# A list scheduler's cost model is rewritten: the same 16,310 instructions in another order

## The chip, the cores and the metric

One program runs on one core of a Trainium2 chip. The metric is the device time of one execution in microseconds (us). The engines are TensorE (PE, its weight loads shown as PEld), VectorE (DVE), ScalarE (ACT), GpSimd (POOL) and SyncE (SP). Each engine works through its own instructions in the order in which the program has them; an instruction whose operands are late holds up all that stand behind it on that engine.

## The reference

One layer over 512 latent tokens and 256 context tokens, width 2048, batch 1. An adaLN-modulated RMSNorm is followed by one input projection, whose columns feed two groups of heads; both groups are gated, joined and sent through one output projection.

```python
mod = silu(c) @ w_ada + b_ada                       # shift, scale, gate; also for c_ctx
xn  = rms(x) * norm_g * (1 + scale) + shift
p   = xn @ w_in                                     # 2048 x 6912 (latent and context rows)
# group A, 16 heads x 64: bidirectional RWKV-7, state S (64 x 64) per head and direction
S   = S * w_t - (S @ kk_t) (kk_t * a_t)^T + v_t k_t^T ;  y_t = S @ r_t
# group B, 16 query / 4 key heads x 64: attention in a window of 128, plus all context keys, one sink
o   = softmax([q k_window, q k_ctx, sink]) @ [v_window, v_ctx]
out = x + gate * (concat(groupnorm(y)*silu(z_r), o*silu(z_a)) @ w_out)
```

## The kernel before

**Tiles and stages.** Tokens lie along the free dimension, channels on the 128 partitions; w_in is cut into 54 column tiles of 128 and w_out into 16. A weight part (4 of a tile's 16 row blocks, 128x512) is loaded into a buffer `wf`, rounded by ACT to `whi`, and DVE writes the rest to `wlo` (`split`); there are two `whi` and two `wlo`. Each of the four blocks then costs three products (whi*xh, whi*xl, wlo*xh), on 512 latent columns and, for the first 22 tiles, on 256 context columns too.
- *Lockstep* (0 to 256 us): w_ada and x arrive, 8 column tiles are projected, the row norms are formed.
- *Context units* (to 610 us): 8 pairs of heads, one unit of 256 tokens each, beside the projection of tiles 8 to 21.
- *Latent units* (to 1322 us): 8 pairs, two units of 256 tokens each, beside the projection of tiles 22 to 53; then the norm and rotary of q and k.
- *Attention* (to 1598 us): 8 pairs of heads, beside the first two quarters and most of the third of the output projection.
- *End*: the fourth quarter, which needs all heads, and 16 finished tiles.

A unit is a chain over the engines: `prep` (decays and scaled keys on POOL, ACT, DVE), `stacks` (64-token products on PE, masked by DVE into `ar`), `relay_out`/`solve` (a triangular system of 31 steps on DVE, with DMAs before and after), `levels` (32x32 and 64x64 products on PE) and `scan`, four steps in which PE, DVE and PE take turns. Matmuls of units use parts of the PE array (modes 32x32, 64x64, 64x128, 128x64), those of projections all of it (128x128).

**What sets the order.** All instructions are first recorded with their dependences (`Program.add`, `touch`). `order` then plays them through a model: each engine has a time at which it is free, each instruction a duration (`estimate`) and a rank (the longest modelled path to the end), and an edge between engines costs `AFTER[p.eng] + BEFORE[o.eng]`. On every engine the ready instruction with the highest rank goes next. The instructions are emitted in the order of their modelled starts, and so the model's numbers fix what stands in front of what.

Projection matmuls are *fills* (`o.fill`): on PE their rank is lowered by `FB`, so that a unit's matmul goes first when it is ready within `LOOK` ns of the first possible start. Five fills in a row (`GRP`) are a group that is kept together. If fewer than `COLMIN` columns were streamed in the last `TICK` ns, a fill goes first. Fills are in a fixed order among themselves. The helper that emits records one line for all: L500 before, L536 after.

Of the kernel before, what the change touches and what calls it, by code (L numbers as in the profile page):

```python
# [183 lines left out]
LAT = BOTH + """  # L184
# [74 lines left out]
class Op:  # L259


    __slots__ = ("n", "eng", "f", "a", "k", "dur", "ldw", "twice", "move", "fill", "group", "prev", "next", "left",
                 "ready", "at", "end", "rank", "cols", "small")


class Area:
# [46 lines left out]
class Program:  # L313
# [19 lines left out]
    def add(self, eng, f, a, k):  # L333
        o = Op()
        o.n, o.eng, o.f, o.a, o.k, o.fill = len(self.ops), eng, f, a, k, self.fill
        o.prev, o.next, o.ready, o.ldw, o.twice, o.move = {}, [], 0.0, 0.0, False, 0.0
# [11 lines left out]
        if eng == "scalar" and f == "dma_start":  # L348
            o.dur = 400
        if eng == "tensor":  # L350
            o.small = bool(k.get("tile_position"))
# [12 lines left out]
    def touch(self, o, ap, write):  # L364
# [4 lines left out]
        for i in area.parts:  # L369
            seen = self.seen.setdefault((ap.name, i), ([], []))  # L370
            for w in (False, True) if write else (True,):
                keep = []
                for n, x in seen[w]:
                    if n != o.n and area.meets(x):
                        p = self.ops[n]
                        if p.eng != o.eng or (w and not write and o.eng != "tensor"):
                            lat = self.AFTER[p.eng] + self.BEFORE[o.eng]
                        else:
                            lat = 0
                        o.prev[n] = max(o.prev.get(n, 0), lat)  # L380
                        own = True
                    if not (write and area.covers(x)):
                        keep.append((n, x))
                seen[w][:] = keep
            seen[write].append((o.n, area))
        if held:
            assert held.next is None, ap.name
            if held.last and not own:
                for n in held.last.users:
                    if n != o.n:  # L390
                        p = self.ops[n]
                        lat = self.AFTER[p.eng] + self.BEFORE[o.eng] if p.eng != o.eng else 0
                        o.prev[n] = max(o.prev.get(n, 0), lat)
            held.users.append(o.n)

    def estimate(self, o, outs, ins):
        f, n = o.f, max(size(x) for x in outs[:1] + ins)
        bank = any(x.space == PSUM for x in ins)
        if o.eng == "sync":
            x = outs[0]  # L400
            some = x.shape[0] == 32 and x.space != DRAM and (size(x) > 256 or len(x.ap) > 2)
            o.dur = 625 if x.shape[0] == 64 or some else 450
            row = int(x.ap[-1][1])
            o.move = max(180, math.prod(x.shape) * 4 / (360 if row >= 128 else 240))
        elif o.eng == "tensor":
            m, n = (size(o.k["lhsT"]), size(o.k["rhs"])) if f == "matmul" else (size(ins[0]), size(ins[1]))
            fast = f == "matmul" and ins[0].dtype != F32
            o.twice = f == "matmul" and not fast
            o.dur, o.ldw = n * (0.417 if fast else 0.834), m * 0.834
            o.cols = n * ins[0].shape[0] / 128 * (2 if o.twice else 1)  # L410
            if self.tied and ins[0].shape[0] == 64:
                o.dur /= 2
                o.ldw /= 2
            if o.k.get("tile_position") and o.twice:
                if m == 32 and n >= 128:
                    o.twice, o.dur = False, 0.417 * n + 21
                else:
                    o.twice, o.dur = False, 0.834 * n + (28 if m == 64 else 10)
        elif o.eng == "vector":
            fast = f in ("tensor_copy", "tensor_scalar") and not bank  # L420
            o.dur = 68 + (0.52 if fast else 1.04) * n
            if (f in ("scalar_tensor_tensor", "tensor_scalar")
                    and any(isinstance(x, bass.AP) and size(x) == 1 for x in o.a[2:])):
                o.dur += 60
        elif o.eng == "scalar":
            o.dur = (52 if bank else 94) + 0.834 * n + (93 if "accum_out" in o.k else 0)
            o.dur += 93 * sum(isinstance(o.k.get(x), bass.AP) for x in ("scale", "bias")) if f == "activation" else 0
        else:
            o.dur = {"memset": 36 + 0.84 * n, "tensor_scalar": 160 + 0.84 * n, "tensor_copy": 125 + 3.3 * n}.get(
                f, 150 + 2.1 * n)  # L430

    def order(self):
        ops = self.ops
        for o in ops:
            for n in o.prev:
                ops[n].next.append(o.n)
            o.left = len(o.prev)
        for o in reversed(ops):
            o.rank = o.dur * (2 if o.twice else 1) + (o.move + 650 if o.move else 0)
            o.rank += max((ops[n].prev[o.n] + ops[n].rank for n in o.next), default=0)  # L440
        free = dict.fromkeys(self.AFTER, 0.0)
        begun = moved = 0.0
        group, small, recent, cols = None, False, deque(), 0.0
        avail = {e: [] for e in free}
        for o in ops:
            if not o.left:
                avail[o.eng].append(o)
        key = lambda o: ((o.eng != "tensor") * o.fill, o.rank - (FB if o.fill and o.eng == "tensor" else 0), -o.n)
        done = 0
        while done < len(ops):  # L450
            t, e = min((max(free[e], min(o.ready for o in l)), e) for e, l in avail.items() if l)
            if e == "tensor":
                for o in avail[e]:
                    o.at = max(free[e], max(begun, o.ready) + o.ldw)
                x = min(o.at for o in avail[e]) + LOOK
# [3 lines left out]
                busy = [o for o in avail[e] if o.fill and o.at <= x + FWAIT] if cols < COLMIN else []  # L459
# [3 lines left out]
                group, small = o.group, o.small  # L463
# [5 lines left out]
            o.at = max(t, o.ready)  # L469
            if e == "tensor":  # L470
                o.at = max(free[e], max(begun, o.ready) + o.ldw)
                begun, o.end = o.at, o.at + o.dur
                if o.twice:
                    begun = max(o.end, o.at + o.ldw)
                    o.end = begun + o.dur
                elif o.k.get("tile_position"):
                    begun = o.end - 20
                free[e] = o.end
            elif e == "sync":
                free[e] = o.at + o.dur  # L480
                moved = max(moved, free[e] + 650) + o.move
                o.end = moved
            else:
                free[e] = o.end = o.at + o.dur
# [18 lines left out]

TICK, COLMIN, FWAIT, FB, LOOK, GRP = 3413, 4000, 0, 80000, 30, 5


class Pool:
# [1204 lines left out]
```

## Time and profile before

| | |
|---|---|
| median of 3 runs | 1680.74 us (1673.76 to 1681.35) |
| profiled execution | 1677.45 us, span 1675.6 us |
| PE / DVE / ACT / POOL busy | 1556.3 (93%) / 1319.0 (79%) / 716.6 (43%) / 404.0 (24%) |
| PE granted clock, mean | 0.98 of full speed |
| matmuls recorded | 12454, of 9288 PE instructions (fp32 ones run as two) |

The share of PE is that of matmul records whose ends are modelled and which overlap, so a wide projection product counts 0.41 us although the next one starts 0.23 us later. Idle time of PE in the trace is therefore only the part of a wait that goes beyond a record's end. Times in rows are from the span's start.

### The profile page before, as it was taken

To read this page: it belongs to the slowest core of one execution; us is meant where nothing else is said; L and a number is where in the kernel's file an instruction comes from. 1 tells how busy PE (TensorE), PEld (TensorE's weight loads), DVE (VectorE), ACT (ScalarE), POOL (GpSimd) and SP (SyncE) were. 2 spreads that over 40 slices of the span, in tenths; PEclk is the share of its full clock that TensorE was granted. 3 is DMA by queue.
4 is the path that set the end of the run, shared out by engine and by line. 5 is a ranking of instruction groups with operands and counts; after the bars stand their busy time and mean duration, and the time that the engine had idled before them with its cause. 6 is when DMAs were issued, how large, how long until landed. Compare 5 with 4: busy or idle time off the path is not lost. (4 is left out here: it accounts for less than half of the span.)

```text
span 1675.6 us, 34264 instructions
## 1 busy us (share of the span) xinstructions
PE 1556.3 (93%) x12454; PEld 1210.9 (72%) x12454; DVE 1319.0 (79%) x3921; ACT 716.6 (43%) x1484; POOL 404.0 (24%) x615
## 2 busy tenths in 40 slices
PE   7998898999999999999998898989888999999998
PEld 5666677878787777777666666767666778788887
DVE  2356889888898846989888898888889558899865
ACT  3432364333343333434443433434333338776723
POOL 2358613010111002122222323123234300111000
PEclk9999998999999999999999999999999999999999
DMA  9976464435444443333333233323343562222146
GB/s 352 332 244 227 123 196 150 129 100 148 118 145 141 139 129 125 116 89 114 107 107 100 92 106 98 100 87 111 89 133 118 170 189 76 76 70 70 45 132 195
DMA packets 215322, 225.78 MB, mean 135 GB/s; under 512 B 78704, under 2 KB 139632, under 8 KB 215152
## 3 DMA queue, kind: packets, MB, share of 16 engines
q1 hardware_dynamic: 181360, 218.86, 41.0%
q10 hardware_dynamic: 33792, 4.73, 1.7%
q8 instruction: 98, 1.61, 0.4%
q14 instruction: 72, 0.59, 0.1%
HBM read 190.49 MB, written 33.03 MB: 133 GB/s over the span
## 5 line engine op out<-in xcount | busy, mean ns | idle before, releaser
L500 PE MATMUL psum<-xh,whi.0_41_283 128*128 128x512 f32 x624 | 242.5, 412 | 1.7 <-DVE xh L500 1.1
L500 PE MATMUL psum<-xh,whi.1_44_313 128*128 128x512 f32 x624 | 240.0, 407 | 0.2 <-ACT xh L500 0.2
L500 PE MATMUL psum<-xh,wlo.0_42_287 128*128 128x512 f32 x528 | 216.3, 410 | 0.0
L500 PE MATMUL psum<-xh,wlo.1_45_325 128*128 128x512 f32 x528 | 215.2, 408 | 0.7 <-DVE wlo.1_45_325 L500 0.7
L500 PE MATMUL psum<-xl,whi.1_44_313 128*128 128x512 f32 x432 | 177.3, 411 | 4.4 <-DVE xl L500 4.4
L500 PE MATMUL psum<-xl,whi.0_41_283 128*128 128x512 f32 x432 | 177.9, 412 | 2.3 <-DVE xl L500 2.2
L500 DVE TENSOR_TENSOR s<-x,nb 128x60 f32<-128x60 f32 (+21 forms) x648 | 156.8, 242 | 10.1
L500 DVE TENSOR_TENSOR x<-x,s 128x60 f32<-128x60 f32 (+21 forms) x648 | 155.6, 240 | 10.6
L500 PEld LDWEIGHTS psum<-xh,whi.0_41_283 128*128 128x128 f32 x624 | 119.0, 192 | 29.6 <-issue 4.1
L500 PEld LDWEIGHTS psum<-xh,whi.1_44_313 128*128 128x128 f32 x624 | 117.8, 190 | 24.7 <-issue 2.9
L500 PEld LDWEIGHTS psum<-xh,wlo.0_42_287 128*128 128x128 f32 x528 | 101.3, 192 | 22.4 <-issue 1.6
L500 PEld LDWEIGHTS psum<-xh,wlo.1_45_325 128*128 128x128 f32 x528 | 100.5, 190 | 22.4 <-DVE wlo.1_45_325 L500 1.5
L500 PEld LDWEIGHTS psum<-xl,whi.0_41_283 128*128 128x128 f32 x432 | 83.4, 193 | 21.4 <-DVE xl L500 4.0
L500 PEld LDWEIGHTS psum<-xl,whi.1_44_313 128*128 128x128 f32 x432 | 82.4, 191 | 22.4 <-DVE xl L500 5.7
L500 ACT COPY uv<-psum 64x128 f32<-64x128 f32 (+2 forms) x103 | 29.1, 282 | 135.0 <-DVE uv L500 70.0
L500 PE MATMUL psum<-kr,bk 64*128 64x128 f32 (+1 forms) x640 | 67.0, 298 | 13.4 <-DVE x L500 4.5
L500 ACT ACTIVATE e<-psum,drv 128x256 f32<-128x256 f32 x96 | 44.4, 476 | 78.5 <-PE psum L500 23.1
L500 PEld LDWEIGHTS psum<-kr,bk 64*128 64x128 f32 (+1 forms) x640 | 54.0, 195 | 29.6 <-issue 10.1
L500 PE MATMUL psum<-uv,ar 64*64 64x64 f32 (+1 forms) x1280 | 71.2, 234 | 1.4 <-ACT uv L500 1.4
L500 PE MATMUL psum<-uv,kb 128*64 128x64 f32 (+1 forms) x848 | 64.9, 244 | 8.0 <-DVE uv L500 7.5
L500 PEld LDWEIGHTS psum<-uv,kb 128*64 128x64 f32 (+1 forms) x848 | 46.8, 141 | 32.5 <-DVE uv L500 13.9
L500 POOL TENSOR_TENSOR s<-s 128x128 f32<-128x128 f32 x56 | 34.8, 622 | 139.8 <-DVE s L500 111.8
(376 smaller groups left out, 3828.2 us busy)
## 6 DMA issues: line engine op xcount, KB each, us to landing
wf.0_40_230<-in_wt_dram SPq DMA_DIRECT2D x72, 256.0 KB, 2.7
wf.1_43_236<-in_wt_dram SPq DMA_DIRECT2D x72, 256.0 KB, 2.8
wf.2_50_248<-in_wt_dram SPq DMA_DIRECT2D x72, 256.0 KB, 2.8
x<-in_wga_dram SPq DMA_DIRECT2D x64, 256.0 KB, 2.8
nb<-it SPq DMA_DIRECT2D x24, 496.0 KB, 4.0
kr<-in_wss_dram SPq DMA_DIRECT2D x22, 512.0 KB, 7.1
kb<-in_wss_dram SPq DMA_DIRECT2D x22, 512.0 KB, 6.0
uv<-dvt SPq DMA_DIRECT2D x48, 128.0 KB, 2.9
```

What stands on the lines that cost most here:

```text
L500: getattr(getattr(self.nc, o.eng), o.f)(*a, **k)
```

## The change

Only the scheduler's model changes; no instruction is added or removed, and each keeps its shape. (1) Edges between engines get one number per pair (`LAT`), to which `order` adds 100 ns if the receiver is PE, 60 ns otherwise and 500 ns after a DMA. (2) `estimate` gets new durations, and DVE, ACT and POOL are free again somewhat before an instruction's end (`over`); DVE and POOL exclude each other for instructions that `lock`. (3) PE gets array modes: a change of mode starts 85 ns after the last matmul's modelled end, weight loads overlap only without one, and each pass of an fp32 matmul is placed by itself. (4) DMAs issued by SP and by ACT get 16 queues, and at most 8 in flight. (5) `FB` goes from 80000 to 1000000, `LOOK` from 30 to 200, `COLMIN` from 4000 to 2900; `GRP` stays 5.

```diff
-    AFTER = {"vector": 127, "scalar": 131, "gpsimd": 76, "tensor": 196, "sync": 905}
-    BEFORE = {"vector": 0, "scalar": 0, "gpsimd": 28, "tensor": 22, "sync": -7}
+    LAT = {"scalar": {"vector": 33, "tensor": 53, "gpsimd": 70, "sync": 27, "scalar": 33},
+           "vector": {"scalar": 36, "tensor": 55, "gpsimd": 80, "sync": 28, "vector": 33},
+           "tensor": {"scalar": 38, "vector": 38, "sync": 40, "gpsimd": 70, "tensor": 0},
...
-            if o.k.get("tile_position") and o.twice:
...
-                    o.twice, o.dur = False, 0.834 * n + (28 if m == 64 else 10)
+            o.mode = (128, 128) if k == 1 else (up(k), up(m) if tiled else 128)
+            o.ldw, o.twice = m / 1.2, single and f == "matmul"
+            if tiled:
+                each = (87 if n >= 128 else 34) if m == 32 else 77 if n <= 64 else 128
+                o.steps = [0, each] if o.twice else [each]
+            elif o.mode == (64, 128):
+                o.steps = [107] * (2 if o.twice else 1)
+            else:
+                each = max(n * (2 if single else 1) / 2.4 + 3 if single else 0.4425 * n + 3, o.ldw + 4.5)
+                o.steps = [each] * (2 if o.twice else 1)
+            o.dur = sum(o.steps)
+            o.tail = max(o.steps[-1], n / 2.4 * (2 if single else 1)) + 172
...
-            o.dur = 68 + (0.52 if fast else 1.04) * n
+            o.dur = 153 + (0.52 if fast else 2.08 if f == "tensor_tensor_scan" else 1.04) * n
+            o.lock, o.over = fast or (two and f != "tensor_reduce"), 81
...
+        def turn(o):
+            t = max(o.ready, loaded, began)
+            return t if mode in (None, o.mode) else max(t, ended + 85)
...
-                    o.at = max(free[e], max(begun, o.ready) + o.ldw)
+                    o.at = max(turn(o) + o.ldw, ended)
                 x = min(o.at for o in avail[e]) + LOOK
-                c = [o for o in avail[e] if o.at <= x]
+                c = [o for o in avail[e] if o.at <= x or o.ready <= t]
...
-                run = [o for o in c if o.small] if small else []
+                run = [o for o in c if o.mode != (128, 128)] if mode != (128, 128) else []
                 o = max(busy or same or run or c, key=key)
...
-                x.ready = max(x.ready, begun if e == x.eng == "tensor" else o.end + x.prev[o.n] +
-                              2000 * (e == "scalar" and o.f == "dma_start"))
+                late = o.end + x.prev[o.n] if x.prev[o.n] else 0
+                if e != x.eng:
+                    late += PEWAIT if x.eng == "tensor" else WAIT
+                if o.f == "dma_start":
+                    late += DMAWAIT
+                x.ready = max(x.ready, late)
...
-TICK, COLMIN, FWAIT, FB, LOOK, GRP = 3413, 4000, 0, 80000, 30, 5
+TICK, COLMIN, FB, LOOK, GRP = 3413, 2900, 1000000, 200, 5
+PEWAIT, WAIT, DMAWAIT = 100, 60, 500
```

What moves can be counted in the two orders of PE. Fills that stand ahead of a unit's last matmul, leaving out the lockstep stage's: context pair 7 1324 before and 1299 now, latent pair 3 2194 and 2239, pair 5 2449 and 2569, pair 7 2719 and 2939; ahead of the last matmul of attention 3369 and 3465, of 3648 in all. Between the first latent unit's and pair 7's last matmul the fills stand in 245 runs before and in 246 now. Changes of array mode from one PE instruction to the next: 1218 before, 1258 now. On SP the first four loads of w_ada stood behind the first load of x and stand ahead of it now.

PE beside pairs 5 and 6 of the latent units, before (`s,q` is the solve's result applied in a scan step, `rz` the products of `levels`, `uv,kb` and `uv,ar` the rest of a step, `kr,bk` the `stacks` of pair 6; `xh` or `xl` with `whi` or `wlo` is a fill):

```order
L500 MATMUL psum<-xh_9_510,whi.1_44_313 128x512
L500 MATMUL psum<-xl_55_520,whi.1_44_313 128x512
L500 MATMUL psum<-s_202,q_1119 64x64 x4
L500 MATMUL psum<-rz_252 64x64 x16
L500 MATMUL psum<-uv_47_239,kb_37_219 64x64 x4
L500 MATMUL psum<-uv_30_232,ar_32_234 64x64 x4
L500 MATMUL psum<-uv_47_239,ar_81_6559 64x64 x4
L500 MATMUL psum<-kr_35_214,bk_244 128x128 x8
```

The same scan step in the changed order:

```order
L536 MATMUL psum<-rz_258 64x64 x16
L536 MATMUL psum<-kr_33_209,bk_246 128x128
L536 MATMUL psum<-xh_6_376,whi.0_41_275 128x512
L536 MATMUL psum<-xl_51_384,whi.0_41_275 128x512
L536 MATMUL psum<-xh_6_376,wlo.0_42_281 128x512
L536 MATMUL psum<-xh_7_405,whi.0_41_275 128x512
L536 MATMUL psum<-xl_53_413,whi.0_41_275 128x512
L536 MATMUL psum<-s_202,q_1137 64x64 x4
L536 MATMUL psum<-kr_33_209,bk_246 128x128 x5
L536 MATMUL psum<-uv_47_236,kb_37_217 64x64 x4
```

`rz` and a group of five fills now stand ahead of `s,q`, and products of pair 6 between `s,q` and `uv,kb`, where `rz` alone stood.

PE at the end of attention, before (`bk,kb` is the last product of the last pair of heads; the `lwl`, `wzl`, `ar` with `whi` or `wlo` are fills of the third quarter of the output projection):

```order
L500 MATMUL psum<-bk_14237,kb_100_14054 128x256
L500 MATMUL psum<-bk_14237,kb_100_14054 64x256
L500 MATMUL psum<-lwl_21_2064,whi.0_41_283 128x512
L500 MATMUL psum<-wzl_1885,whi.0_41_283 128x512
L500 MATMUL psum<-lwl_21_2064,wlo.0_42_287 128x512
L500 MATMUL psum<-ar_101_13972,whi.1_44_313 128x512
```

The same place in the changed order (`xh` is a fill of the fourth quarter):

```order
L536 MATMUL psum<-bk_14362,kb_100_14097 128x256
L536 MATMUL psum<-bk_14362,kb_100_14097 64x256
L536 MATMUL psum<-xh_7_405,whi.0_41_275 128x512
L536 MATMUL psum<-xh_16_751,whi.0_41_275 128x512
L536 MATMUL psum<-xh_7_405,wlo.0_42_281 128x512
L536 MATMUL psum<-xh_3_279,whi.1_44_310 128x512
```

The third quarter has moved in front of the end of attention as a whole.

## Rows read from the trace of the kernel before

**Rows 1.** Windows by stage: busy us of each engine (and instructions), clock, DMA share, GB/s.

```profile
0.00:256.00 256.00, 226.66 (x1516) 169.54 (x1516) 151.79 (x263) 104.61 (x195) 123.44 (x132) 0.96 0.73 244
256.00:610.00 354.00, 338.86 (x3030) 275.38 (x3030) 296.96 (x1026) 131.30 (x285) 42.35 (x88) 0.99 0.45 134
610.00:1322.00 712.00, 650.73 (x5994) 485.92 (x5991) 608.74 (x2137) 278.65 (x579) 207.67 (x374) 0.98 0.36 109
1322.00:1598.00 276.00, 267.39 (x1577) 220.98 (x1577) 218.36 (x431) 178.85 (x386) 30.49 (x22) 1.00 0.29 94
```

**Rows 2.** Waits of PE in the latent units: us, times, longest.

```profile
PE psum L500 <- DVE x L500: 19.8, 15, 3.0
```

**Rows 3.** Timeline of PE beside latent pairs 5 and 6: start, us, operation, idle before.

```profile
1108.29 0.40 PE L500 MATMUL psum<-xh,whi.0_41_283 128*128 128x512 f32 x1
1108.61 0.62 PE L500 MATMUL psum<-uv,kb 128*64 128x64 f32 x8
...
1110.67 0.50 PE L500 MATMUL psum<-xl,whi.0_41_283 128*128 128x512 f32 x1
1111.01 0.39 PE L500 MATMUL psum<-xh,wlo.0_42_287 128*128 128x512 f32 x1
...
1115.50 0.45 PE L500 MATMUL psum<-s,q 64*64 64x64 f32 x8 [0.69 <-DVE s L500]
...
1118.01 0.45 PE L500 MATMUL psum<-uv,kb 128*64 128x64 f32 x8 [0.93 <-DVE uv L500]
```

**Rows 4.** Windows for the tiles whi.0, whi.1, wlo.0, wlo.1 alone, latent units.

```profile
610.00:1322.00 712.00, 158.47 (x460) 86.04 (x461) 41.63 (x58) 35.28 (x57) 0.98 0.36 109
610.00:1322.00 712.00, 161.50 (x469) 86.92 (x469) 42.20 (x58) 35.95 (x58) 0.98 0.36 109
610.00:1322.00 712.00, 95.66 (x230) 44.28 (x230) 41.63 (x58) 0.98 0.36 109
610.00:1322.00 712.00, 96.50 (x235) 45.01 (x235) 42.20 (x58) 0.98 0.36 109
```

**Rows 5.** Timeline of PE: end of latent pair 7.

```profile
1322.28 0.60 PE L500 MATMUL psum<-kon,p 128*128 128x128 f32 x4
```

**Rows 6.** Timeline of PE: end of attention.

```profile
1597.98 0.63 PE L500 MATMUL psum<-bk,kb 128*128 128x256 f32 x4
1598.45 0.40 PE L500 MATMUL psum<-lwl,whi.0_41_283 128*128 128x512 f32 x1
...
1603.82 0.40 PE L500 MATMUL psum<-ar,wlo.0_42_287 128*128 128x512 f32 x1
```

**Rows 7.** Chain of waits, its last parts: start, us, engine.

```profile
1560.51 109.09 PE psum L500 x573
...
1671.25 0.64 PE psum L500 x4
```

**Rows 8.** Windows of 100 us.

```profile
300.00:400.00 100.00, 97.55 (x838) 80.45 (x837) 83.69 (x303) 39.29 (x86) 14.33 (x27) 0.98 0.43 125
...
1200.00:1300.00 100.00, 85.46 (x818) 62.50 (x819) 90.41 (x393) 36.58 (x73) 34.87 (x41) 0.95 0.39 120
```

**Rows 9.** Waits of DVE in the latent units.

```profile
DVE wlo.0_42_287 L500 <- ACT whi.0_41_283 L500: 13.6, 16, 2.4
...
DVE wlo.1_45_325 L500 <- ACT whi.1_44_313 L500: 13.0, 9, 4.2
```

**Rows 10.** Waits of DVE in attention.

```profile
DVE wlo.0_42_287 L500 <- ACT whi.0_41_283 L500: 14.9, 10, 2.1
DVE wlo.1_45_325 L500 <- ACT whi.1_44_313 L500: 14.2, 7, 4.2
```

**Rows 11.** Timeline of all engines at one collision.

```profile
1092.07 0.79 POOL L500 TENSOR_TENSOR bk<-p,e 128x256 f32<-128x256 f32 x1 [0.36 <-DVE p L500]
1092.25 0.68 DVE L500 TENSOR_TENSOR x<-x,s 128x49 f32<-128x49 f32 x1
...
1093.41 0.20 DVE L500 TENSOR_TENSOR x<-x,s 128x42 f32<-128x42 f32 x1
```

More of the change, by code (lines that the diff above doesn't have):

```diff
@@ L259 @@
 class Op:
-    __slots__ = ("n", "eng", "f", "a", "k", "dur", "ldw", "twice", "move", "fill", "group", "prev", "next", "left",
-                 "ready", "at", "end", "rank", "cols", "small")
+    __slots__ = ("n", "eng", "f", "a", "k", "dur", "long", "over", "lock", "ldw", "steps", "tail", "mode", "twice", "move",
+                 "load", "queues", "fill", "group", "prev", "next", "left", "ready", "at", "end", "rank", "cols")
 class Area:
@@ L335, in add @@
         o.n, o.eng, o.f, o.a, o.k, o.fill = len(self.ops), eng, f, a, k, self.fill
-        o.prev, o.next, o.ready, o.ldw, o.twice, o.move = {}, [], 0.0, 0.0, False, 0.0
+        o.prev, o.next, o.ready = {}, [], 0.0
         aps = [x for x in a if isinstance(x, bass.AP)]
@@ L375, in touch @@
                         p = self.ops[n]
[L376 to L380, printed above, removed]
+                        wait = p.eng != o.eng or o.eng == "sync" or (w and not write and o.eng != "tensor")
+                        o.prev[n] = max(o.prev.get(n, 0), self.LAT[p.eng][o.eng] if wait else 0)
                         own = True
@@ L432, in order @@
+            o.over = 96
+        else:
+            o.dur = {"memset": 105 + 0.84 * n, "tensor_scalar": 195 + 0.84 * n, "tensor_copy": 185 + 1.25 * n}.get(
+                f, 195 + 2.15 * n)
+            o.lock, o.over = f != "memset", 42
+        if o.eng not in ("sync", "tensor") and f != "dma_start":
+            o.long = o.dur
     def order(self):
@@ L438, in order @@
         for o in reversed(ops):
-            o.rank = o.dur * (2 if o.twice else 1) + (o.move + 650 if o.move else 0)
+            o.rank = o.dur if o.eng == "tensor" and all(ops[n].eng == "tensor" for n in o.next) else o.long
             o.rank += max((ops[n].prev[o.n] + ops[n].rank for n in o.next), default=0)
-        free = dict.fromkeys(self.AFTER, 0.0)
-        begun = moved = 0.0
-        group, small, recent, cols = None, False, deque(), 0.0
+        free = dict.fromkeys(self.LAT, 0.0)
+        loaded = began = ended = cols = 0.0
+        mode = group = None
+        held, queues, recent, lanes = {"vector": 0.0, "gpsimd": 0.0}, [0.0] * 16, deque(), deque()
         avail = {e: [] for e in free}
@@ L453, in order @@
                 for o in avail[e]:
-                    o.at = max(free[e], max(begun, o.ready) + o.ldw)
+                    o.at = max(turn(o) + o.ldw, ended)
                 x = min(o.at for o in avail[e]) + LOOK
-                c = [o for o in avail[e] if o.at <= x]
+                c = [o for o in avail[e] if o.at <= x or o.ready <= t]
                 while recent and recent[0][0] < x - TICK:
                     cols -= recent.popleft()[1]
-                busy = [o for o in avail[e] if o.fill and o.at <= x + FWAIT] if cols < COLMIN else []
+                busy = [o for o in c if o.fill] if cols < COLMIN else []
                 same = [o for o in c if o.group == group]
-                run = [o for o in c if o.small] if small else []
+                run = [o for o in c if o.mode != (128, 128)] if mode != (128, 128) else []
                 o = max(busy or same or run or c, key=key)
-                group, small = o.group, o.small
+                group = o.group
+                for i, x in enumerate(o.steps):
+                    loaded = turn(o) + o.ldw
+                    began = ended if i and o.k.get("tile_position") else max(loaded, ended)
+                    o.at = o.at if i else began
+                    mode, ended = o.mode, began + x
+                o.end = began + o.tail
+                free[e] = began - 50
                 recent.append((o.at, o.cols))
@@ L467, in order @@
                 o = max((o for o in avail[e] if o.ready <= t), key=key)
-            avail[e].remove(o)
[L469 to L484, printed above, removed]
+                o.at = t
+                if o.f == "dma_start":
+                    if len(lanes) == 8:
+                        o.at = t = max(t, lanes.popleft() + 50)
+                    x = t + o.dur
+                    for i in range(o.queues):
+                        queues[i] = max(queues[i], x + 700) + o.move
+                    o.end = max(x + o.tail, max(queues[:o.queues]) + 450)
+                    lanes.append(o.end)
+                    free[e] = x + 60
+                else:
+                    o.end = max(t, held["gpsimd" if e == "vector" else "vector"] if o.lock else 0) + o.dur
+                    if o.lock:
+                        held[e] = o.end - 150
+                    free[e] = o.end - o.over
+            avail[e].remove(o)
             for n in o.next:
                 x = ops[n]
-                x.ready = max(x.ready, begun if e == x.eng == "tensor" else o.end + x.prev[o.n] +
-                              2000 * (e == "scalar" and o.f == "dma_start"))
+                late = o.end + x.prev[o.n] if x.prev[o.n] else 0
+                if e != x.eng:
+                    late += PEWAIT if x.eng == "tensor" else WAIT
+                if o.f == "dma_start":
+                    late += DMAWAIT
+                x.ready = max(x.ready, late)
                 x.left -= 1
```

74 lines of the change are left out of this document (42 added, 32 removed).

## The prediction

> **What bounds the kernel now.** I read the windows by stage first, then the waits of TensorE and VectorE in the longest stage, then TensorE's timeline at single places and the end of the chain of waits. The windows show TensorE busy in every stage and no stage free of idle time: 29.3 us idle in the lockstep stage, 15.1 in the context units, 61.3 of 712 us in the latent units and 8.6 of 276 in attention [rows 1]. VectorE stands just below it, 608.7 of 712 us in the latent units (85%) and 218.4 of 276 in attention (79%). So two engines are near their limit at the same time, and each waits for the other where the order was wrong: TensorE's waits in the latent units are mostly for VectorE, 15 of them for the units' `x` alone [rows 2].
>
> The reader is to see one thing in the chain of waits: from 1560.51 us it is nothing but 573 matmuls, 109 us, and then one transposition [rows 7]. The kernel ends on a stock of projection work that ran alone, while earlier TensorE had stood idle. Projections that are moved from that stock into earlier idle time are a gain; projections moved in front of a matmul that was ready are none.
>
> **The change part by part.** Nothing is added or removed, so the sum is over what moved. It is made against the profiled execution, 1677.45 us, which lies between the lowest run (1673.76) and the median (1680.74); I apply no correction. A projection product of 512 columns costs what separates two starts: 24 of them begin between 1598.45 and 1603.82, 5.37 us for 23 steps, 0.2335 us each [rows 6]. The recorded 0.40 us is not that price, since records overlap.
>
> *After attention.* Its last matmul starts at 1598.3 (fourth of the four from 1597.98) and 279 of 3648 fills are then left; in the new order 183 are. 96 fewer times 0.2335 is -22.4 us. Nothing runs beside these except the finishing of tiles, so this is certain if attention does not end later.
>
> *Latent pair 7 to the end of attention.* Pair 7's last transpositions are at 1322.28 [rows 5]. From there to the end of attention stood 650 fills, now 526: 124 fewer, 29.0 us of a stage in which TensorE was busy 267.4 of 276 us. VectorE sheds 10 weight parts (12 products each) at 0.72 us (41.63 us for 58, [rows 4]), 7 us, which leaves 211 us; in 247 us that is 85%, and 90% is the highest share that any 100 us show [rows 8]. Its waits for weight rounding, 29.1 us here [rows 10], do not vanish with it; I give back 5 us and count -24. The bounds are -29 and 0.
>
> *The latent units.* The fills between the first latent one and pair 7's end go from 1375 to 1595 (the windows count 1394 matmuls on the four weight tiles between 610 and 1322 us, [rows 4]). 220 more are 51.4 us of work, and 61.3 us were idle. If all of it lands in idle time the stage keeps its length, if none does it grows by 51.4. For where they land: the place in the first pair of pieces of the order is one at which TensorE sat idle 0.69 us before `s,q` and 0.93 before `uv,kb` [rows 3], and a group of fills and other products stand there now. The number of runs of fills is unchanged (245, 246), so the runs got longer, and no more of them break in. By busy time, 650.7 + 51.4 is 702.1 us, and the best 100 us beside units show 97.55% [rows 8]: 720 us. Against that stands the clock. It is granted at 0.98 over the stage, and since its levels are 1.2 and 2.4 GHz this is 4% or 28 us at the lower one [rows 1], which costs 14 us of busy time; fills in the place of waits should give some two thirds of it back, 9.5. (702.1 - 9.5) / 0.9755 is 710 us, -2. The bounds are -24 (VectorE's, first rival) and +51.4.
>
> *Array modes.* The changes of mode go from 1218 to 1258. In the rows a narrow matmul follows a wide one after 0.32 us in place of 0.2335, and the first wide one after a narrow one holds the next back for 0.34 [rows 3]: 0.09 and 0.11 us. 40 more are +4 us. The bounds are 0 and +10, as some of them fall into waits. The Trainium skill speaks against the change here: "TensorEngine Tiling (Array Packing)", Key Properties, says that a change of tiling mode drains the engine. By the row the drain is only the 0.09 us; if each took a full recorded product of 0.40 us, the term would be 16 us and the sum 12 us higher.
>
> *Lockstep and context units.* The fills hardly move (1324 to 1299 at context pair 7's end), and the loads of w_ada go ahead of the first x load. The trace has nothing of the other order of loads. The gain is bounded by the idle time of both stages, 44 us; for a loss I take as much as the context stage has idle, 15 us. I take 0, since the waits there are for loads and for VectorE in turn and neither the loads nor the operations get fewer.
>
> Sum: 1677.45 - 22.4 - 24 - 2 + 4 = 1633 us, 2.8% below.
>
> **The rivals.** *VectorE sets the latent units.* If the new order removes nearly all unplanned waits, the stage shrinks until VectorE is full: 608.7 us and 18 more weight parts of 0.72 (13.2) are 621.9, and at the highest share seen, 90.4% [rows 8], that is 688 us, -24. With a quarter of the 44 us of the early stages: 1677.45 - 22.4 - 24 - 24 + 4 - 11 = 1600 us. For it: the latent waits come from an order that left them uncovered, and fills are at hand all the time. Against it: an engine with 90% in one window and 85% in the stage needs every operation on time, and some VectorE operations are stretched by GpSimd: 0.68 us for an `x` update beside a GpSimd operation of 0.79, 0.20 us for a like one a microsecond later [rows 11]. The Trainium skill, "SBUF — State Buffer", section on the two separate sides, has the port that both use as an exclusive lock for a whole instruction. The row agrees: the operation ends when GpSimd's does. By that rule the 608.7 us hold such waits, and another order beside GpSimd can lower or raise this rival's floor.
>
> *The fills stand on the chain.* If the 220 fills all delay ready matmuls, the work only changes places: 1677.45 - 22.4 - 24 + 51.4 + 4 = 1686 us, no change to slightly slower. For it: fills come in groups of five, 1.2 us, ahead of matmuls whose waits are 0.7 and 0.9 [rows 3]. Against it: 61.3 us of idle time would have to stay as they are.
>
> *VectorE's queue, the slower side.* The split of each weight part (`wlo`) stands in VectorE's queue among the units' operations and waits for ACT's rounding, which waits for a free `whi`, that is for the fills before. When TensorE is behind the plan, this wait holds everything behind it. In the latent units it cost 26.6 us for 116 parts, 0.23 each [rows 4, 9]; in attention 29.1 us for 55, 0.53 each [rows 10] (55 is 652 fills over 12, rounded up). At 0.53 the 134 parts of the new stage wait 71 us, 44 more, and if half of the added fills, 25 us, also delay the chain, the stage grows by 69: 1677.45 - 22.4 - 24 + 69 + 4 = 1704 us. It decides from a growth of 42 us on, where the gains of the two later stages are used up. For it: more parts in the same time, and an engine at 85%. Against it: the latent units have the lower price although they are the busier stage.
>
> **How the numbers follow.** The forecast has 0.56, with a range of its own of 1612 to 1660 (the latent units may miss their value by some 20 us either way, and the rest by a few); VectorE's limit 0.20, fills on the chain 0.10, VectorE's queue 0.14. What a measurement of this kernel can tell from no change is about 0.5%, 8 us. Faster takes the first two, 0.76; the third lies at that margin, 0.10 for no change; slower 0.14. The range reaches down past the first rival to 1596, as the early stages may give more than a quarter, and up to 1685, where the second rival ends; what is left out is most of the third and the lower tail, 2 in 10.
>
> **What would show it.** Right: pair 7's last transpositions within 15 us of 1322 with some 1600 fills before them in that stage, TensorE's idle time there under 30 us, its waits for `x` and `s` about halved, the clock at 0.99; some 252 us from there to the end of attention; about 51 us after it. Wrong in the step of the latent units: pair 7 ends after 1360 us, or VectorE's waits of `wlo` for `whi` in that stage pass 50 us. Wrong in the step of attention: TensorE idle over 25 us there. If the first 610 us change by more than 15, the step that I set to 0 was the one that mattered.

## The result and the profile after

The changed kernel takes 1694.27 us (median of 4 runs, 1691.23 to 1702.2), the kernel before 1677.76 (4 runs): ratio 1.0106, 95% interval 1.0082 to 1.013. It is about 1.1% slower where 2.8% faster was forecast, and above the range that was given. The profiled execution took 1695.21 us, span 1693.2, mean granted clock 0.98.

I place the stages by the starts of their last matmuls, as in [rows 5, 6]: the latent units end at 1387.1 us (1322.6 before), attention at 1632.8 (1598.3), the last matmul starts at 1689.2 (1671.6). The windows of the changed kernel, cut at its own ends of stages (the columns are those of [rows 1]):

```profile
0.00:237.00 237.00, 219.76 (x1508) 164.01 (x1509) 156.96 (x250) 100.83 (x186) 119.90 (x125) 0.99 0.76 259
237.00:615.00 378.00, 342.65 (x3016) 275.45 (x3015) 300.14 (x1039) 133.84 (x293) 47.96 (x95) 0.98 0.44 126
615.00:1387.00 772.00, 716.98 (x6239) 534.70 (x6240) 633.09 (x2161) 290.99 (x607) 202.37 (x373) 0.98 0.38 112
1387.00:1633.00 246.00, 240.48 (x1450) 199.14 (x1447) 206.56 (x424) 170.07 (x368) 33.36 (x24) 0.99 0.26 80
1633.00:1694.00 61.00, 51.73 (x248) 41.48 (x247) 33.05 (x51) 18.27 (x31) 0.00 (x0) 0.95 0.58 171
```

Lockstep lost 19 us (256 to 237), the context units gained 24 (354 to 378), the latent units gained 60 (712.6 to 772.4), attention lost 30 (276 to 246), the rest lost 17. TensorE's idle time in the latent units is 55.0 us, where 61.3 stood [rows 1]: 66 us more busy time, 60 us more time in all. The four weight tiles in that stage, against [rows 4], in the order whi.0, whi.1, wlo.0, wlo.1:

```profile
615.00:1387.00 772.00, 187.25 (x550) 101.50 (x550) 50.65 (x67) 41.47 (x68) 0.98 0.38 112
615.00:1387.00 772.00, 182.96 (x544) 100.52 (x544) 49.62 (x68) 41.28 (x67) 0.98 0.38 112
615.00:1387.00 772.00, 112.04 (x274) 52.53 (x274) 50.65 (x67) 0.98 0.38 112
615.00:1387.00 772.00, 111.51 (x272) 52.05 (x272) 49.62 (x68) 0.98 0.38 112
```

That is 1640 fills (projection matmuls) in place of 1394. TensorE's two largest waits in this stage (us, times, longest; the first answers to [rows 2]):

```profile
PE psum L536 <- DVE x L536: 13.6, 24, 2.7
PE psum L536 <- DVE s L536: 8.8, 9, 2.2
```

The wait for `x` fell from 19.8 us to 13.6 and stands at 24 places in place of 15. VectorE's waits there (the two of `wlo` answer to [rows 9]):

```profile
DVE wlo.0_42_281 L536 <- ACT whi.0_41_275 L536: 22.1, 17, 4.1
DVE uv L536 <- PE psum L536: 17.3, 10, 4.2
DVE wlo.1_45_330 L536 <- ACT whi.1_44_310 L536: 15.1, 15, 2.0
DVE rz L536 <- DMA x<-iw: 14.2, 14, 2.1
DVE x L536 <- DMA nb<-it: 11.0, 10, 3.0
```

The two `wlo` sum to 37.2 us, up from 26.6. How fills and waits stand side by side shows in a stretch of TensorE's timeline (start, us, operation, idle before):

```profile
1142.55 0.33 PE L536 MATMUL psum<-uv,ar 64*64 64x64 f32 x4
1142.81 0.50 PE L536 MATMUL psum<-xh,whi.1_44_310 128*128 128x512 f32 x1
...
1143.84 0.40 PE L536 MATMUL psum<-xl,whi.1_44_310 128*128 128x512 f32 x1
1144.17 0.33 PE L536 MATMUL psum<-uv,ar 64*64 64x64 f32 x4
1144.43 0.44 PE L536 MATMUL psum<-x,kr 128*64 128x128 f32 x4
1146.00 0.69 PE L536 MATMUL psum<-rz,ar 32*32 32x32 f32 x32 [1.14 <-DVE rz L536]
1146.63 0.49 PE L536 MATMUL psum<-kr,bk 64*128 64x128 f32 x2
1147.04 0.50 PE L536 MATMUL psum<-xh,wlo.1_45_330 128*128 128x512 f32 x1
...
1148.39 0.48 PE L536 MATMUL psum<-kr,bk 64*128 64x128 f32 x2
1148.81 0.49 PE L536 MATMUL psum<-xl,whi.0_41_275 128*128 128x512 f32 x1
```

Five fills run, two kinds of unit product follow, and TensorE stands still for 1.14 us until VectorE has `rz` ready. The awaited product and one `kr,bk` run, and then five fills come again. After them a `kr,bk` stands alone between two groups of five: a group for one short product, and two changes of array mode. The end of the kernel is shorter, as forecast; the last product of attention and the first fill after it, and the chain of waits behind them, against [rows 6, 7]:

```profile
1632.23 0.83 PE L536 MATMUL psum<-bk,kb 128*128 128x256 f32 x4
1635.87 0.50 PE L536 MATMUL psum<-xh,whi.0_41_275 128*128 128x512 f32 x1 [2.81 <-DVE xh L536]
```

```profile
1636.60 50.56 PE psum L536 x242
1687.91 0.76 DVE p L536
```

### The profile page after: what moved, and what is told of

Its sections match the earlier page's. It is cut to its first block, busy times and chain, and to the rows that moved or that the text cites. A ratio compares the mean times of both kernels' runs of the same rounds, so it can differ in the third digit from the quotient of the medians.

```text
span 1693.2 us, 34324 instructions
## 1 busy us (share of the span) xinstructions
PE 1571.6 (93%) x12454; PEld 1214.8 (72%) x12454; DVE 1329.8 (79%) x3921; ACT 714.0 (42%) x1484; POOL 403.6 (24%) x615
## 4 chain that ended last, share of the span: by engine, by line
DVE 29%; PE 25%; DMA 9%; issue 4%; ACT 2%; POOL 1%; ACTq 1%; SPq 0%; DVEq 0%; POOLq 0%
PE psum L536 25%; DVE s L536 8%; DVE x L536 7%; DMA iw<-x 3%; DVE e L536 2%; DVE ar L536 2%; DVE wlo.1_45_330 L536 2%; DVE wlo.0_42_281 L536 2%; DMA x<-iw 2%; DVE kk L536 1%; DVE p L536 1%; DVE uv L536 1%; DMA nb<-it 1%; DVE bk L536 1%; DMA x<-in_wga_dram 1%
## 5 line engine op out<-in xcount | busy, mean ns | idle before, releaser
L536 DVE TENSOR_TENSOR s<-x,nb 128x60 f32<-128x60 f32 (+21 forms) x648 | 152.1, 235 | 9.7
L536 DVE TENSOR_TENSOR x<-x,s 128x60 f32<-128x60 f32 (+21 forms) x648 | 149.5, 231 | 10.1
L536 PE MATMUL psum<-uv,kb 128*64 128x64 f32 (+1 forms) x848 | 71.3, 247 | 12.6 <-DVE uv L536 11.7
L536 PE MATMUL psum<-uv,ar 64*64 64x64 f32 (+1 forms) x1280 | 77.9, 233 | 3.9 <-DVE uv L536 3.6
L536 PEld LDWEIGHTS psum<-uv,ar 64*64 64x64 f32 (+1 forms) x1280 | 56.4, 136 | 21.8 <-issue 5.2
L536 PE MATMUL psum<-kon,p 128*128 128x128 f32 x392 | 60.9, 278 | 8.7 <-DVE p L536 4.5
```

Source lines behind the costliest of these rows:

```text
L536: getattr(getattr(self.nc, o.eng), o.f)(*a, **k)
```

## A ledger for all runs

To compare orders I split TensorE's time. The distance from each matmul's start to the next has a usual size for that kind of pair of neighbours (shape, and whether parts of the array are used): its median over the traces of the two kernels. The sum of these is the *price* of an order, with its changes of mode; what a distance has beyond its median is *delay*. Stages in us by the same ends as above; medians of runs; delay also for the context (c), latent (l) and attention (a) stages alone. All columns but the median are of the profiled execution, which was 9 us shorter than the median in e9, 5 shorter in e5 and 7 longer in e11. How the time divides depends somewhat on how fine the kinds are: with matmuls that start within 30 ns of each other taken as one, the latent stage's price rises by 66 us from before to after and its delay falls by 6, where the table's ledger has 61.5 and 1.

| run | median | lockstep, context, latent, attention, end | mode changes | price | delay | c / l / a |
|---|---|---|---|---|---|---|
| before | 1678 | 256, 354, 713, 276, 73 | 1218 | 1442 | 224 | 36 / 102 / 21 |
| after | 1694 | 237, 378, 772, 246, 56 | 1258 | 1447 | 236 | 64 / 101 / 20 |
| e1 | 1896 | 239, 601, 751, 246, 56 | 1233 | 1449 | 439 | 98 / 232 / 54 |
| e2 | 1721 | 249, 356, 726, 300, 85 | 1209 | 1438 | 272 | 52 / 134 / 28 |
| e3 | 1723 | 236, 387, 772, 257, 66 | 1280 | 1452 | 261 | 78 / 116 / 20 |
| e4 | 1707 | 239, 377, 788, 244, 56 | 1271 | 1445 | 253 | 41 / 108 / 52 |
| e5 | 1687 | 237, 361, 737, 278, 64 | 1159 | 1425 | 245 | 63 / 119 / 18 |
| e6 | 1681 | 237, 379, 738, 257, 64 | 1215 | 1433 | 235 | 60 / 110 / 20 |
| e7 | 1656 | 235, 367, 736, 256, 56 | 1168 | 1426 | 217 | 53 / 99 / 18 |
| e8 | 1701 | 251, 362, 719, 287, 73 | 1216 | 1440 | 245 | 40 / 125 / 21 |
| e9 | 1666 | 237, 367, 720, 272, 56 | 1156 | 1422 | 224 | 54 / 111 / 13 |
| e10 | 1666 | 242, 367, 727, 266, 56 | 1152 | 1423 | 229 | 54 / 109 / 13 |
| e11 | 1692 | 236, 379, 776, 246, 56 | 1266 | 1444 | 244 | 44 / 98 / 51 |
| e12 | 1684 | 241, 367, 770, 241, 56 | 1186 | 1207 | 463 | 57 / 303 / 48 |
| e13 | 1680 | 234, 375, 718, 281, 64 | 1257 | 1446 | 221 | 62 / 98 / 17 |
| e14 | 1650 | 239, 375, 726, 247, 57 | 1171 | 1423 | 214 | 46 / 88 / 29 |

Read the first two lines: the later stages gained 47 us and the latent one took 60, but no matmul was added. By the ledger the kernel is 5.8 us dearer in price and 12.4 in delay, 18 in all: lockstep's delay fell by 18 us, the context units' rose by 28, that of the latent units stayed.

## The experiments

The first theories were A: a fill costs its full time wherever it stands, waits stay, so moving fills is worth nothing; B: the new selection constants made the loss; C: waits are lateness against the plan, and slack covers it.

**e1, the old constants in the new model.** Ratio 1.1297 (1.1266 to 1.1328).

```diff
-TICK, COLMIN, FB, LOOK, GRP = 3413, 2900, 1000000, 200, 5
+TICK, COLMIN, FB, LOOK, GRP = 3413, 4000, 80000, 30, 5
```

> The changed kernel with the selection constants of before (FB 80000, LOOK 30, COLMIN 4000); the new durations, edges, array modes and lanes stay. Fills ahead of latent pair 7's end go from 2939 to 3081 of 3648 and ahead of context pair 7's end from 1299 to 2134. Theory A (a latent or context unit pays every fill beside it in full, because the waits stay): the context stage grows by about 835 x 0.2335 = 195 us less whatever idle it had, the latent stage shrinks by about 693 x 0.2335 = 160, the total stays within 10 us of the changed kernel, 1684 to 1704. Theory B (the constants made the loss): 1670 to 1680.

Both missed, by far. 2134 fills stood ahead of context pair 7's end in place of 1299, and the latent units then had too few (947 in place of 1640); TensorE's clock fell there to 0.81, a mean over its levels of 1.2 and 2.4 GHz:

```profile
840.00:1591.00 751.00, 642.52 (x5565) 474.65 (x5563) 605.33 (x2102) 260.56 (x550) 196.25 (x373) 0.81 0.31 88
```

`COLMIN` 4000 doesn't mean in the new model what it meant in the old one: there a narrow product counted all its columns, now only its part of the array's width. So this run tells of the force of the constants and not of theory B. That `COLMIN` is the one at work is argued and not shown, as `FB` and `LOOK` change too.

**e2, the new constants in the old model.** Ratio 1.0238 (1.0189 to 1.0287).

```diff
-TICK, COLMIN, FWAIT, FB, LOOK, GRP = 3413, 4000, 0, 80000, 30, 5
+TICK, COLMIN, FWAIT, FB, LOOK, GRP = 3413, 2900, 0, 1000000, 200, 5
```

> The kernel before with the three new constants alone (FB 1000000, LOOK 200, COLMIN 2900), old durations and edges. Fills ahead of latent pair 7's end fall from 2719 to 2599. Theory A: the latent stage gets about 120 x 0.2335 = 28 us shorter and the rest 28 us longer, the total stays within 10 us of before, 1668 to 1688. Theory B (the constants made the loss): 1690 or more.

B has the direction and A misses: the constants alone cost 42 us, all of it delay, most of that in the latent units (102 to 134).

**e3 and e4, no slack and three times the slack.** Ratios 1.0273 (1.0237 to 1.0308) and 1.0169 (1.014 to 1.0198).

```diff
-PEWAIT, WAIT, DMAWAIT = 100, 60, 500
+PEWAIT, WAIT, DMAWAIT = 0, 0, 0          # e3
+PEWAIT, WAIT, DMAWAIT = 300, 180, 1500   # e4
```

> The changed kernel without the slack on edges (PEWAIT, WAIT, DMAWAIT all 0). Fills ahead of latent pair 7's end 2834 in place of 2939. Theory A: latent stage 25 us shorter than the changed kernel's 772, the rest 25 us longer, total 1684 to 1704. Theory C (waits are lateness against the plan, and slack covers it): TensorE's waits in the latent units rise above 70 us and the total above 1705.

> The changed kernel with three times the slack on edges (PEWAIT 300, WAIT 180, DMAWAIT 1500). Fills ahead of latent pair 7's end 3081, the most that can stand there. Theory A: latent stage longer by about what it holds more, total 1684 to 1710. Theory C: TensorE's waits in the latent units fall below 35 us (from 54) and the total below 1680.

e3's total came as C says, though TensorE idled 64 us in the latent units, where C said over 70. e4 came as A says: it idled 55 us there, where C said under 35. C is half right. Delay in the context units falls with slack, 78, 64 and 41 us (e3, after, e4). But a plan with more slack shows more idle time and fills it: 1414 fills ahead of context pair 7, 3081 ahead of latent pair 7, so that attention had only 384, its delay rose from 20 to 52 us, and its clock fell to 0.94.

The next four ask for the rule on columns (if fewer than `COLMIN` were streamed lately, a fill goes first, even ahead of a ready unit product). D: this rule, made stricter by the new count, costs the latent units. E: it keeps the clock up and its absence costs more.

**e5, no column rule in the changed kernel.** Ratio to before 1.0049 (1.0025 to 1.0073).

```diff
-TICK, COLMIN, FB, LOOK, GRP = 3413, 2900, 1000000, 200, 5
+TICK, COLMIN, FB, LOOK, GRP = 3413, 0, 1000000, 200, 5
```

> The changed kernel with COLMIN 0 in place of 2900: no fill goes ahead because few columns were counted. 2729 fills stand ahead of latent pair 7's end (2939 with the rule, 2719 in the kernel before). Theory D (the column rule, whose count became stricter, puts fills in front of ready unit products): the latent stage falls from 772 to 715-735 us and the whole to 1660-1680. Theory A (a fill is paid in full wherever it stands, waits stay): the stage falls by about 49 us (210 fills of 0.2335) and the later ones grow as much; whole 1685-1705. Theory E (the rule keeps the clock up): granted clock under 0.95, whole over 1700.

**e6, the old count of columns.** Ratio 1.0012 (0.9992 to 1.0032).

```diff
-                o.cols = n * min(k, 128) * m / 128 / 128 * (2 if single else 1)
+                o.cols = n * k / 128 * (2 if single else 1)
```

> The changed kernel with the column count of the kernel before (a narrow unit product counts all its columns, not by the part of the array's width), threshold 2900 kept: the rule steps in less often. 2834 fills ahead of latent pair 7's end. D: half of the way, latent stage 735-755 us, whole 1665-1685. A: 1685-1705. E: as the changed kernel, clock 0.97-0.98, 1690-1705.

**e7, no rule, LOOK 30, half more slack.** Ratio 0.986 (0.9819 to 0.9901).

```diff
+TICK, COLMIN, FB, LOOK, GRP = 3413, 0, 1000000, 30, 5
+PEWAIT, WAIT, DMAWAIT = 150, 90, 750
```

> The changed kernel with COLMIN 0, LOOK 30 and slacks 150/90/750 (half more). 2884 fills ahead of latent pair 7's end, all but 183 ahead of attention's end. D: nothing forces a fill and the waits are better covered, 1640-1670. A: as many fills in the latent stage as before the edit less 55, so 1680-1705. E: clock under 0.95, over 1700.

**e8, no rule in the kernel before.** Ratio 1.0149 (1.0116 to 1.0182).

```diff
-TICK, COLMIN, FWAIT, FB, LOOK, GRP = 3413, 4000, 0, 80000, 30, 5
+TICK, COLMIN, FWAIT, FB, LOOK, GRP = 3413, 0, 0, 80000, 30, 5
```

> The kernel before with COLMIN 0 in place of 4000. 2669 fills ahead of latent pair 7's end (2719 with the rule). D: the rule costs less there (its count was looser), 1660-1676. A: 1672-1685, no change. E: clock under 0.95 and over 1690.

E fell: with COLMIN 0 the clock stays at 0.977 to 0.982 in all three kernels without the rule. D has the direction for the stage: 772 us become 737, 738 and 736, where it said 715 to 735 for the first and 735 to 755 for the second. For the whole its ranges hold in e6 and e7, not in e5 and e8; e5's whole, 1687 us, lies in A's range. In e5 the price falls by 22 us (99 fewer changes of mode), but the latent delay rises by 18, and 7 us are left; in e7 the delay doesn't rise, and 38 are left. In the old model the rule helps: without it, delay rises by 21. The latent units of e5:

```profile
597.00:1334.00 737.00, 670.91 (x6114) 510.28 (x6114) 616.75 (x2136) 281.30 (x586) 197.22 (x372) 0.97 0.36 108
```

**e9 and e10, the parts of e7; e11, e7 with the rule.** Ratios 0.9924 (0.9896 to 0.9951), 0.9944 (0.9921 to 0.9966), 1.0085 (1.0056 to 1.0113).

```diff
-TICK, COLMIN, FB, LOOK, GRP = 3413, 0, 1000000, 30, 5
+TICK, COLMIN, FB, LOOK, GRP = 3413, 0, 1000000, 200, 5       # e9, against e7
-PEWAIT, WAIT, DMAWAIT = 150, 90, 750
+PEWAIT, WAIT, DMAWAIT = 100, 60, 500                         # e10, against e7
-TICK, COLMIN, FB, LOOK, GRP = 3413, 0, 1000000, 30, 5
+TICK, COLMIN, FB, LOOK, GRP = 3413, 2900, 1000000, 30, 5     # e11, against e7
```

> The changed kernel with COLMIN 0 and slacks 150/90/750, LOOK 200 kept. Against the run without the rule (1687 us) only the slack differs, against the one with LOOK 30 too (1656 us) only LOOK. Theory F (slack covers lateness, above all of VectorE in the context units): 1655-1670. Theory G (LOOK 200 lets TensorE wait up to 0.2 us for a unit's product that isn't ready, and the gain was LOOK's): 1675-1690.

> The changed kernel with COLMIN 0 and LOOK 30, slacks 100/60/500 kept. F: 1675-1690. G: 1655-1668. Both in part: 1664-1676.

> The changed kernel with LOOK 30 and slacks 150/90/750, the column rule (2900) kept. 3069 fills ahead of latent pair 7's end. Theory D (the rule's forced fills cost the latent stage some 35 us): latent stage 765-785 us, whole 1685-1705, against 1656 without the rule. If slack and LOOK alone made the gain: 1655-1670.

Slack and `LOOK` each give some 21 us without the rule (1687 to 1666), both together 31, and with the rule 2 (1694 to 1692). So F and G hold each in part, and D's price for the rule holds: e11 and e7 differ in the rule alone, 36 us (43 between their profiled executions). In the latent units the rule puts 1670 fills in place of 1562, and they take 40 us more; the 108 fills are 25 us of that at 0.2335, and delay is the same (98, 99). Latent units and attention of e11, and of e7:

```profile
615.00:1391.00 776.00, 724.67 (x6296) 539.51 (x6295) 644.91 (x2179) 300.53 (x625) 204.55 (x376) 0.98 0.37 112
1391.00:1637.00 246.00, 220.82 (x1299) 180.67 (x1296) 198.95 (x398) 156.91 (x341) 29.17 (x20) 0.95 0.22 69
```

```profile
602.00:1337.00 735.00, 681.98 (x6158) 514.03 (x6157) 632.43 (x2161) 287.95 (x598) 201.64 (x374) 0.98 0.39 115
1337.00:1593.00 256.00, 252.35 (x1509) 211.36 (x1509) 215.32 (x425) 174.43 (x376) 31.25 (x22) 0.99 0.28 87
```

With the rule attention has 396 fills left and TensorE idles 25 us at clock 0.95; without it 581 are left, and 3.6 us idle at 0.99. By the ledger the rule costs 18 us of price (98 changes of mode) and 34 us of delay in attention, whose stock it has used up; it gives back 8 in the context units.

**e12, one of three products.** Ratio 1.0037 (1.0019 to 1.0055).

```diff
+                    if n and pc is None:
+                        continue
```

> The changed kernel with one of the three products (the rounded weights times xh) for the projection tiles of the latent and attention stages; leaves out the two other products, so 1024 of 3648 fills are gone; the weight loads, roundings and splits stay. About 773 fills are left in the latent stage in place of 1640. Theory A (a fill is paid in full, the stage is bound by TensorE): 867 times 0.2335 is 202 us less, latent stage 570-600 us. Theory U (the chain of the units over VectorE and the DMAs bounds the stage, fills lie mostly beside it): latent stage 700-750 us.

**e13, no low part for latent tiles.** Ratio 1.002 (1.0004 to 1.0037).

```diff
+        if not low:
+            nc.scalar.copy(hi, src)
+            return hi, hi
```

> The changed kernel without the split on VectorE for the 32 tiles of latent rows only: their third product takes the rounded weights a second time in place of the low part; leaves out 128 VectorE operations of 0.7 us (92 us) and the low part of those weights; as many matmuls as the changed kernel. Theory V (VectorE, with the units' chain through it, sets the latent stage): stage 700-735 us and whole 1640-1670. Theory P (TensorE with the fills put in front sets it): the rule and the fills stay, stage 755-775, whole 1680-1697.

Latent units of e12, then of e13:

```profile
607.00:1378.00 771.00, 611.54 (x5387) 443.42 (x5386) 644.59 (x2185) 308.36 (x632) 198.23 (x375) 0.79 0.39 117
```

```profile
610.00:1328.00 718.00, 665.69 (x6006) 496.26 (x6007) 538.60 (x1993) 272.87 (x575) 179.90 (x366) 0.98 0.36 106
```

A's stage of 570 to 600 us did not come in e12: with 773 fills in place of 1640 the stage keeps its length, 770 against 772 us, and TensorE idles 160 us in it. That speaks for U, but the stage is also longer than U's 700 to 750. One doubt stays: the clock there fell to 0.79, and how much of the 202 us of missing work the slower clock ate, this run doesn't part.

In e13 VectorE is 92 us lighter and the rule is the same, and the stage falls by 54 us, to 718, within V's range. But the order is another one too: the plan puts 1420 fills beside the units, 220 fewer, and these are 51 us at 0.2335. TensorE idles 52 us in the stage, where it idled 55, and its delay is 98, where it was 101. So e13 shows that with less VectorE work the plan is done with the units sooner and puts fewer fills beside them. It doesn't part the units' chain through VectorE from the price of the fills, and that the chain alone sets the stage's length isn't shown. The other 220 fills move behind the units, attention and the end grow by 43 us, and the whole falls by 15, where V expected 24 at least. A is right as a ledger of the whole.

**e14, twice the slack.** Ratio 0.985 (0.9824 to 0.9876), 1650.34 us.

```diff
+TICK, COLMIN, FB, LOOK, GRP = 3413, 0, 1000000, 30, 5
+PEWAIT, WAIT, DMAWAIT = 200, 120, 1000
```

> The changed kernel with COLMIN 0, LOOK 30 and slacks 200/120/1000. 2964 fills ahead of latent pair 7's end. Theory F (more slack covers more lateness): lateness in the context units under 50 us (52 at 150/90/750) and the whole 1645-1656. Theory P (more slack is more idle time in the plan, which takes more fills early and has none left in attention): 1660-1680.

F holds: 46 us of delay in the context units, and P's loss in attention is only 11 us (18 to 29). It beats both kernels, as e7 does; the two are not told apart by their intervals. Its context and latent windows, TensorE's wait for `x` and VectorE's for `whi` there:

```profile
239.00:613.00 374.00, 353.90 (x3098) 288.01 (x3097) 306.02 (x1038) 136.57 (x297) 48.18 (x95) 0.99 0.46 133
613.00:1340.00 727.00, 680.36 (x6181) 510.35 (x6181) 643.55 (x2166) 290.95 (x606) 207.28 (x374) 1.00 0.40 117
```

```profile
PE psum L536 <- DVE x L536: 8.3, 16, 1.6
```

```profile
DVE wlo.0_42_281 L536 <- ACT whi.0_41_275 L536: 8.2, 12, 1.3
DVE wlo.1_45_331 L536 <- ACT whi.1_44_312 L536: 7.6, 7, 2.0
```

The two `wlo` waits are 15.8 us, against 37.2 in the changed kernel. With 1570 fills in the latent units it has nearly as many as the changed kernel (1640), in 726 us. Against the kernel before these are some 175 fills more, 41 us at 0.2335, but the stage is only 13 us longer: delay there is 14 us lower and the whole order has 47 fewer changes of mode. So fills can find room beside the units, in another order.

## Why the prediction was wrong

**After attention, and attention itself: right in sum, in part by luck.** -17 and -30 us came for -22.4 and -24, together -47 for -46. Two misses cancel. The end was called certain, since nothing runs beside it but the finishing of tiles. But in the old order fills of the third quarter stood behind attention's last product; now TensorE waits 2.81 us for `xh` there, as the row above shows, and in the next 8 us, with fills alone, the granted clock is 0.79:

```profile
1637.00:1645.00 8.00, 8.00 (x32) 6.39 (x31) 3.99 (x7) 2.10 (x4) 0.00 (x0) 0.79 0.25 82
```

Attention gained 1 us more than its bound of -29. VectorE's waits for weight rounding, for which I gave back 5 us, fell there from 29.1 us to 7.3; the rows that answer to [rows 10]:

```profile
DVE wlo.1_45_330 L536 <- ACT whi.1_44_310 L536: 4.9, 5, 1.6
...
DVE wlo.0_42_281 L536 <- ACT whi.0_41_275 L536: 2.4, 6, 0.8
```

**The latent units: the step that failed.** It set the stage at -2 by letting 220 fills land in 61.3 us of idle time. The stage grew by 60. In the ledger 61.5 us of that are price (246 fills of 0.2335 are 57; some 31 changes of mode come on top), and the delay stayed, 102 to 101. TensorE idled 55.0 us, where under 30 was forecast. The 9.5 us that the clock was to give back did not come either: it was granted at 0.98 in this stage before and after. The failed inference was from busy times: that 650.7 us and 51.4 fit into a stage because 97.55% was once seen, and that in a stage of context units. The idle time consists mostly of waits for VectorE; the timeline above shows 1.14 us of it between two groups of five fills that did not fill it. Before I asked where fills land, I should have asked what sets the length of the stage.

What the runs show of that is the column rule. Leaving aside e1 and the two runs with less work (e12, e13): where the rule counts in the new way (after, e3, e4, e11), the stage has 772 to 788 us and 1570 to 1670 fills. Without it in the new model (e5, e7, e9, e10, e14) it has 720 to 737 us and 1455 to 1570 fills, and with the old count (e6) 738. The number of fills alone doesn't set the length: e3 and e14 both have some 1570 and differ by 46 us. e11 and e7, which differ in the rule alone, differ by 40. By how much the units' chain over VectorE sets it as well stays open, as said at e12 and e13. My reason that runs of fills got longer and no more of them break in was no protection: by the trace, a unit product that comes right after a run of fills was ready 158 us before its start in sum (from the run's start at the earliest; 215 runs) before, 177 (225 runs) after, 96 in e5 and 122 in e7. That sum is no price by itself, as the kernel before has 158 in a stage of 713 us. Without the rule the new model's units are still 7 to 24 us longer than those of the kernel before, but they have 60 to 175 more fills beside them, which are 14 to 41 us at 0.2335.

**The second rival had the right arithmetic.** 220 fills at full price, and "61.3 us of idle time would have to stay": 55.0 did. It gave 1686, and the context units, price and 25 more fills make up the rest. The slower rival named VectorE's queue; its mark, `wlo` waits past 50 us, was not reached (37.2), its growth of the stage was (60 past 42), by another cause. VectorE's limit as a gain fell.

**Lockstep and context units: 0 forecast, +5 came, of two parts.** Lockstep, where the loads of w_ada now go ahead of x, became 19 us shorter (that order was not tried by itself); the context units became 24 longer, with 28 more of delay. VectorE's waits there, before and then after:

```profile
DVE wlo.1_45_325 L500 <- ACT whi.1_44_313 L500: 3.4, 4, 1.6
DVE wlo.0_42_287 L500 <- ACT whi.0_41_283 L500: 2.0, 3, 1.5
```

```profile
DVE wlo.1_45_330 L536 <- ACT whi.1_44_310 L536: 9.8, 6, 3.4
DVE rz L536 <- DMA x<-iw: 7.8, 5, 3.4
```

The bound of a loss there (15 us, as much as the stage has idle) was too small: an order can lose more than it had idle. With slack alone changed, delay there is 78, 64 and 41 us at 0, 1 and 3 times the change's (e3, after, e4), which speaks for lateness against the plan as its cause. It is not the only one: with the rule off and `LOOK` 30, half more slack changes nothing (54 and 53 in e10 and e7), and `LOOK` 30 in place of 200 takes off 9 us by itself (63 in e5, 54 in e10).

**Array modes: right in kind.** +4 was forecast for 40 changes, 0.10 us each; the price of the whole order rose by 5.8. The price of e11 and e7, with the same matmuls, differs by 18 us for 98 changes, 0.18 each; after and e5 give 22 for 99. With matmuls that start within 30 ns taken as one, the two differences are 8 and 14 us, so a change costs 0.1 to 0.2 us here, and the runs don't tell it closer. "TensorEngine Tiling (Array Packing)" of the Trainium skill, Key Properties, says that a change of mode drains the engine. These runs agree that it costs time; they don't show by what.

**The percentage.** The sum, 1633 us, is 2.6% below the profiled execution that it starts from (1677.45); the 2.8% is against the median of 1680.74.

## What to carry to other kernels

When a scheduler moves filler work and removes none, count the whole first: price of the work on the fullest engine plus its delay; a stage that loses filler gets shorter and another gets longer, and the whole gains only what price or delay falls. Idle time beside a dependent chain isn't free room: ask what ends it, and what sets the chain's length, before counting on it. Slack, lookahead and the threshold for taking filler must be tuned together: from the changed kernel the threshold alone gave 0.4%, slack and lookahead without it 0.1%, all of them 2.6%.

## What was not expected of the hardware

TensorE's clock needed no rule: with `COLMIN` 0 it was granted at 0.98 (e5, e7) and 0.99 (e14) over the kernel. Its lowest values over a long stage stand where few fills were left beside the units (0.79 in e12, 0.81 in e1), and TensorE idled 160 and 108 us there. And VectorE 92 us lighter (e13) went with a longest stage shorter by 54 us, with 220 fewer fills in it, but with a kernel shorter by only 15.
